# A decoder layer on TensorE: head pairs of the self-attention in three visits instead of four, and projection blocks handed out as they end

## The chip, the cores and the metric

The kernel runs on one core of a Trainium2 chip. The metric is the device time of one execution in microseconds, as the median of several runs; beside it stands one execution recorded by the hardware profiler. TensorE (PE) does the matmuls, VectorE (DVE) and ScalarE (ACT) the element-wise work, GpSimd (POOL) little, and SyncE (SP) issues the loads of weights.

## The reference

One trunk layer for 256 tokens of width 1024. What matters for the change:

```python
x = x + 0.5 * swiglu(rms_norm(x, g_ffn1), w_ffn1_gu, w_ffn1_down)
h = rms_norm(x, g_mix)
q, k, v = split(h @ w_in)                 # two groups: 12 heads dilated windows, 4 heads block-sparse
ya, yb = rms_norm(attention of each group)
x = x + concatenate([ya, yb]) @ w_out
# cross attention, 4 heads of width 256, over 256 memory tokens
q = rms_norm(x, g_cross) @ w_cq;  k, v = split(rms_norm(mem, g_mem) @ w_ckv)
s = einsum('bshe,bmhe->bhsm', q, k) * 256 ** -0.5
x = x + (softmax(s) @ v) @ w_co
x = x + 0.5 * swiglu(rms_norm(x, g_ffn2), w_ffn2_gu, w_ffn2_down)
return rms_norm(x, g_final)
```

With 256 tokens both kinds of self-attention come down to a causal softmax with a table of bias per head.

## The kernel before

Activations lie transposed: features on the partitions, 256 tokens along the free dimension. Every product is done in a split form: a number is a high part and a low part (the rest), both in a fast format, and a product is high x high, high x low and low x high. A weight tile of 128 x 1024 is loaded by SyncE and split by ScalarE (L125, the high part) and then VectorE (L126, the low part, which reads the high one). An activation tile is split the same way by `split` (L318 on ScalarE, L319 on VectorE).

`projT` computes a projection transposed, in blocks of 128 output features. A block takes a bank of TensorE's accumulator memory (eight banks, handed round as they come free) and pairs of input tiles: two matmuls of 512 columns (L224) and two of 256 (L228) a step. It returns the list of its banks when all blocks are done, and the caller then evicts them: `halves` adds the two halves of a bank with ScalarE (L275) and VectorE (L276).

TensorE's order is the order of the program. So that TensorE has work while a softmax runs on the other engines, the program has a clock of its own: each matmul adds an assumed time (`tick`), `later(delay, fn)` puts a piece of attention into a list, and it is written out between two matmuls of a projection as soon as this clock passes its due time. ScalarE's, VectorE's and GpSimd's orders are made by a scheduler.

Self-attention has two groups of eight heads. `attend(g)` handles a group as four pairs of heads (j = 0 to 3): `products` (scores, L516), `softmax`, `turn` (six transpositions of the weights, L555, copied out at L559 and L561) and `pv` (weights times values, L572, copied out at L575, squared for the norm at L348). Group 0 is laid over the projections of group 1 (`qkv(1)`), group 1 over the keys and values of cross attention (`cross_k`, `cross_v`). The pairs come in four visits: scores 0, 1; scores 2 with values 0; scores 3 with values 1; values 2, 3.

Cross attention: `cross_qp` computes Q in two halves of four blocks (c = 0, 1) and queues the four heads' scores (L188, L189, L190, 256 columns); `turn` transposes the weights (L706); `cross_o(h)` multiplies by the values. The output projection `addT(w_co)` starts between them: its `order` names which steps stand ahead of `cross_o(2)` and `cross_o(3)`.

Of the kernel before, what the change touches and what calls it, by code (L numbers as in the profile page):

```python
# [9 lines left out]
F32 = mybir.dt.float32  # L10
# [6 lines left out]
P = 128  # L17
# [3 lines left out]
FF = 2816  # L21
# [7 lines left out]
def layer_kernel(ctx, tc, x_in, mem_in, g_ffn1, w_gu1, w_dn1, g_mix, w_in, rel_bias, g_out_a, g_out_b,  # L29
# [16 lines left out]
    def slot(dt=F32R):  # L46
        return slp.tile([P, 1024], dt, tag="slot", name="slot")
# [83 lines left out]
    def colchunk(wd, c0, n, nkt=KT):  # L131

        per = 1024 // n
        res = []
        for k0 in range(0, nkt, per):
            nk = min(per, nkt - k0)
            w = wload((lambda raw, nk=nk: raw[:, :nk * n].rearrange("p (a n) -> p a n", n=n),
                       cols(wd, k0, nk, c0, n), nk * n))
            res += [(w, i * n) for i in range(nk)]
        return res  # L140
# [17 lines left out]
    def later(delay, fn, *args):  # L158
        events.append((clock[0] + delay, len(events_seq), fn, args))
        events_seq.append(0)  # L160
        events.sort(key=lambda e: e[:2])
# [80 lines left out]
    def projT(wk, xs, nblk, spread=False, whole=0, abreast=False):  # L242

        res = [bank() for _ in range(nblk)] if spread or abreast else []
        if spread and whole:
            res = [b[:, :256] for b in res]
            for k in range(KT):
                mmT_wide(res, wk, xs, k, k == 0, k == KT - 1)
            return res
        if spread:  # L250
            for k in range(KT):
                mmT_run([(res[blk], k, blk) for blk in range(nblk)], wk, xs, 0, KT - 1)
            return res
        if abreast:
            for b0 in range(0, nblk, 2):
                for k in range(0, KT, 2):
                    for blk in (b0, b0 + 1):
                        mmT_run([(res[blk], k, blk), (res[blk], k + 1, blk)], wk, xs, 0, KT - 1)
            return res
        for blk in range(nblk):  # L260
            b = bank()
            if blk >= nblk - whole:
                b = b[:, :256]
                for k in range(KT):
                    mmT(b, wk, xs, k, blk, k == 0, k == KT - 1)
            else:
                for k in range(0, KT, 2):
                    mmT_run([(b, k, blk), (b, k + 1, blk)], wk, xs, 0, KT - 1)
            res.append(b)
        return res  # L270

    def halves(out, ps):

        t = work.tile([P, 256], F32, tag="sq", name="hv", bufs=3)
        nc.scalar.activation(t, ps[:, 256:], AF.Copy)  # L275
        nc.vector.tensor_tensor(out, ps[:, :256], t, OP.add)  # L276
# [136 lines left out]
    def gate_up(w_gu, xs, st, hooks=(), first=None):  # L413
        hid = []
        for c in range(6):
            n = 512 if c < 5 else 256
            nb = n // P
            if c == 0 and first:
                pg, pu = first
            else:  # L420
                pg = projT(colchunk(w_gu, c * 512, n), xs, nb, spread=(c == 0))
                pu = projT(colchunk(w_gu, FF + c * 512, n), xs, nb)
            sil = []
            for b0 in range(0, nb, 2):
                g = work.tile([P, 512], F32, tag="g1", name="g1", bufs=3)
                scaled(g, pg[b0:b0 + 2], st.rows())
                nc.scalar.activation(g, g, AF.Silu)  # L427
                sil.append(g)
            for b0 in range(0, nb, 2):
                u = work.tile([P, 512], F32, tag="u1", name="u1")  # L430
                scaled(u, pu[b0:b0 + 2], st.rows())
                nc.vector.tensor_tensor(u, u, sil[b0 // 2], OP.mult)  # L432
                s = slot()
                hid.append(s)
                split(s, 0, 2, u)
            if c < len(hooks) and hooks[c] is not None:
                later(0.0, hooks[c])
        return hid
# [66 lines left out]
    def attend(g, q, k, v, OT, every, done, wait=1.0):  # L505


        pts, pTs = {}, {}

        def products(j):  # L510
            o = j * 256
            rows = (slice(0, 64), slice(64, 128))
            sp = [bank(), bank()]
            for c, n, t in ((0, 128, 0), (128, 256, 128)):
                for e in range(2):
                    nc.tensor.matmul(sp[e][:, c:c + n], q[rows[e], o + t:o + t + 128], k[rows[e], o:o + n],  # L516
                                     start=True, stop=True)
            tick(0.6)
            return sp

        def scores(js):
            sps = [products(j) for j in js]
            if js[0] > 1:
                pv(js[0] - 2)
            for j, sp in zip(js, sps):
                softmax(j, sp)
                later(12.0 if j == 1 else 8.0, turn, j)

        def softmax(j, sp):
            pts[j] = []  # L530
            for e in range(2):
                h = g * 8 + j * 2 + e
                pt = work.tile([P, 384], F32, tag="pt", name="pt", bufs=4)
                mx = small.tile([P, 2], F32, tag="mx", name="mx")
                nm = small.tile([P, 2], F32, tag="nm", name="nm")
                l = small.tile([P, 2], F32, tag="l", name="l")
                rl = small.tile([P, 2], F32, tag="rl", name="rl")
                for tb, c, n, fo in ((0, 0, 128, 128), (1, 128, 256, 0)):
                    nc.vector.tensor_tensor_reduce(pt[:, c:c + n], sp[e][:, c:c + n], F[h // 8][:, h % 8, fo:fo + n],
                                                   1.0, -3.0e38, OP.add, OP.max, mx[:, tb:tb + 1])  # L540
                nc.vector.tensor_scalar(nm, mx, -1.0, None, OP.mult)
                for tb, c, n in ((0, 0, 128), (1, 128, 256)):
                    nc.scalar.activation(pt[:, c:c + n], pt[:, c:c + n], AF.Exp, bias=nm[:, tb:tb + 1],
                                         accum_out=l[:, tb:tb + 1])
                nc.vector.reciprocal(rl, l)
                for tb, c, n in ((0, 0, 128), (1, 128, 256)):
                    nc.gpsimd.tensor_scalar(pt[:, c:c + n], pt[:, c:c + n], rl[:, tb:tb + 1], 1.0, OP.mult, OP.mult)
                pts[j].append(pt)

        def turn(j):  # L550
            pTs[j] = []
            for e in range(2):
                tp = bank()
                for i in range(3):
                    nc.tensor.transpose(tp[:, i * P:(i + 1) * P], pts[j][e][:, i * P:(i + 1) * P], ident)  # L555
                tick(0.33)
                pT = work.tile([P, 384], F32, tag=("pT", "u1")[e], name="pT", bufs=2)
                if e == 0:
                    nc.vector.tensor_copy(pT, tp[:, :384])  # L559
                else:  # L560
                    nc.scalar.activation(pT, tp[:, :384], AF.Copy)  # L561
                pTs[j].append(pT)
            if j == 3:
                later(3.2, pv, 2)
                later(3.2, pv, 3)

        def pv(j):
            op = bank()[:, :256]
            for kb, c, n in ((0, 0, 256), (1, 256, 128)):
                for e in range(2):  # L570
                    vc = kb * 512 + (j * 2 + e) * 64
                    nc.tensor.matmul(op[e * 64:e * 64 + 64, 256 - n:256], v[:, vc:vc + 64], pTs[j][e][:, c:c + n],  # L572
                                     start=kb == 0, stop=kb == 1)
            tick(0.65)
            nc.vector.tensor_copy(OT[g][:, j * 256:j * 256 + 256], op)  # L575
            done(g * 4 + j, op)

        for js, t in (((0, 1), 0.0), ((2,), 2 * every), ((3,), 2 * every + 5.0)):
            later(wait + t, scores, js)

    def out_split(OT, R, js, ot):

# [67 lines left out]
    def cross_k(ms):  # L650
        K = []
        for c in range(2):
            pieces = projT(colchunk(w_ckv, c * 512, 512), ms, 4)
            for b0 in (0, 2):
                t = work.tile([P, 512], F32, tag="g1", name="kn", bufs=3)
                for i in range(2):
                    halves(t[:, i * 256:i * 256 + 256], pieces[b0 + i])
                s = slot()
                split(s, 0, 2, t)
                K.append(s)  # L660
        return K

    V = [[None, None], [None, None]]
# [78 lines left out]
    xs = [slot() for _ in range(4)]  # L742
# [225 lines left out]
```

## Time and profile before

| | before |
|---|---|
| median of 3 runs | 610.15 us (609.44 to 610.66) |
| the profiled execution | 609.78 us, its span 607.8 us |
| granted TensorE clock, mean | 0.998 of 2.4 GHz |
| TensorE matmuls busy | 596.1 us, 98% of the span |
| VectorE busy | 434.6 us, 72% |
| ScalarE busy | 348.1 us, 57% |
| GpSimd busy | 51.6 us, 8% |

The span is what the profiler saw from the first instruction to the last; the time has some 2 us around it. Busy shares are means over stages that differ, so a stage is read from its own rows.

### The profile page before, as it was taken

The page shows a single profiled execution, that of the slowest core. Times are in us where ns is not written, and L with a number is a line of the kernel's source. Part 1 is how long each engine was busy: PE and PEld are TensorE (multiplying, and loading weights), DVE is VectorE, ACT ScalarE, POOL GpSimd, SP SyncE. Part 2 cuts the span into 40 slices and gives each one's busy share as a digit, 9 for nine tenths or more (in the row PEclk, how much of TensorE's full clock was granted, in tenths as well). Part 3 has the DMA queues.
Part 4 walks back from the last instruction along what each step waited for, and adds up shares of the span by engine and source line. Part 5 has one row for each costly group of instructions (what it writes and reads, how often), then busy time and mean ns, then how long its engine had stood idle before and what let it go on. Part 6 is the DMA issues. An engine that isn't in the chain of part 4 may idle for free.

```text
span 607.8 us, 9496 instructions
## 1 busy us (share of the span) xinstructions
PE 596.1 (98%) x3528; PEld 518.6 (85%) x3528; DVE 434.6 (72%) x730; ACT 348.1 (57%) x606; POOL 51.6 (8%) x83
## 2 busy tenths in 40 slices
PE   8999999999999999999999999899999999999995
PEld 8988888888899888888788899788888888888885
DVE  4889657887666766765797786858888787794424
ACT  6856536655645667656675565647654664654313
POOL 0000200000111102212401120003000000000000
PEclk9999999999999999999999999999999999999999
DMA  7877997677576717444445654543565566476401
GB/s 236 288 227 237 211 221 234 192 245 241 156 242 207 232 56 233 139 139 140 139 127 192 202 160 152 144 133 106 173 223 171 196 201 213 143 268 196 157 0 69
DMA packets 58989, 110.02 MB, mean 181 GB/s; under 512 B 3760, under 2 KB 14608, under 8 KB 58944
## 3 DMA queue, kind: packets, MB, share of 16 engines
q1 hardware_dynamic: 57664, 105.49, 55.1%
q0 software_dynamic: 832, 2.88, 2.8%
q10 hardware_dynamic: 448, 1.05, 0.5%
q8 instruction: 27, 0.44, 0.3%
q14 instruction: 18, 0.15, 0.1%
HBM read 107.58 MB, written 1.84 MB: 180 GB/s over the span
## 4 chain that ended last, share of the span: by engine, by line
PE 94%; DVE 2%; ACT 1%; DMA 1%; issue 1%; SPq 0%; POOLq 0%; POOL 0%; DVEq 0%
PE bank L224 43%; PE bank L228 21%; PE bank L188 7%; PE bank L190 7%; PE bank L189 7%; PE bank L238 4%; PE bank L516 1%; DMA raw<-in_w_ffn_gu_dram 1%; PE bank L555 1%; PE bank L572 1%; DVE w L126 1%; ACT w L125 1%; DVE slot L319 0%; PE bank L380 0%; PE bank L870 0%
## 5 line engine op out<-in xcount | busy, mean ns | idle before, releaser
L224 PE MATMUL bank<-slot,w 128*128 128x512 f32 x1130 | 355.0, 396 | 1.0 <-DVE slot L319 1.0
L126 DVE TENSOR_TENSOR w<-raw,w 128x1024 fp32r<-128x1024 f32 (+1 forms) x197 | 237.3, 1219 | 80.5 <-ACT w L125 79.3
L125 ACT ACTIVATE w<-raw 128x1024 fp32r<-128x1024 f32 (+1 forms) x197 | 202.5, 1051 | 89.4 <-PE bank L190 38.8
L228 PEld LDWEIGHTS bank<-slot,w 128*128 128x128 f32 x1130 | 209.7, 188 | 48.2 <-issue 0.7
L228 PE MATMUL bank<-slot,w 128*128 128x256 f32 x1130 | 221.7, 279 | 0.0
L224 PEld LDWEIGHTS bank<-slot,w 128*128 128x128 f32 x1130 | 174.2, 189 | 4.4 <-issue 1.3
L188 PE MATMUL bank<-w,slot 128*128 128x512 f32 (+1 forms) x156 | 60.5, 388 | 0.0
L190 PE MATMUL bank<-w,slot 128*128 128x512 f32 (+1 forms) x156 | 59.9, 384 | 0.0
L189 PE MATMUL bank<-w,slot 128*128 128x512 f32 (+1 forms) x156 | 59.9, 384 | 0.0
L275 ACT ACTIVATE hv<-bank 128x256 f32<-128x256 f32 x108 | 39.7, 376 | 34.0 <-PE bank L228 33.7
L190 PEld LDWEIGHTS bank<-w,slot 128*128 128x128 f32 x156 | 29.3, 188 | 6.0
L188 PEld LDWEIGHTS bank<-w,slot 128*128 128x128 f32 x156 | 29.3, 188 | 5.9 <-issue 0.3
L189 PEld LDWEIGHTS bank<-w,slot 128*128 128x128 f32 x156 | 29.3, 188 | 5.5
L238 PE MATMUL bank<-slot,w 128*128 128x256 f32 x240 | 31.6, 287 | 0.8 <-ACT w L125 0.7
L318 ACT ACTIVATE slot<-u 128x512 fp32r<-128x512 f32 x22 | 13.8, 629 | 32.0 <-DVE u L432 32.0
L238 PEld LDWEIGHTS bank<-slot,w 128*128 128x128 f32 x240 | 29.5, 191 | 1.7 <-ACT w L125 0.9
L353 POOL TENSOR_TENSOR ssq<-ssq,sq 128x256 f32<-128x256 f32 x22 | 19.5, 886 | 72.0 <-ACT sq L348 71.7
L322 DVE SCALAR_TENSOR_TENSOR slot<-X,gT,slot 128x256 fp32r<-128x256 f32 x30 | 19.4, 659 | 6.9 <-ACT slot L321 6.9
L427 ACT ACTIVATE g<-g 128x512 f32<-128x512 f32 x22 | 13.8, 631 | 18.4 <-DVE g L290 18.4
L276 DVE TENSOR_TENSOR u<-bank,hv 128x256 f32<-128x256 f32 x40 | 16.8, 421 | 9.9 <-ACT hv L275 9.8
L276 DVE TENSOR_TENSOR g<-bank,hv 128x256 f32<-128x256 f32 x40 | 16.5, 420 | 9.0 <-ACT hv L275 9.0
L321 ACT ACTIVATE slot<-X,gT 128x256 fp32r<-128x256 f32 x30 | 14.8, 506 | 13.0 <-DVE X L301 13.0
(129 smaller groups left out, 494.0 us busy)
## 6 DMA issues: line engine op xcount, KB each, us to landing
raw<-in_w_ffn_gu_dram SPq DMA_DIRECT2D x88, 512.0 KB, 4.7
raw<-in_w_ffn_down_dram SPq DMA_DIRECT2D x44, 512.0 KB, 4.6
raw<-in_w_ckv_dram SPq DMA_DIRECT2D x16, 512.0 KB, 6.0
raw<-in_w_in_dram SPq DMA_DIRECT2D x12, 512.0 KB, 3.8
raw<-in_w_in_dram SPq DMA_DIRECT2D x24, 256.0 KB, 4.4
raw<-in_w_out_dram SPq DMA_DIRECT2D x8, 512.0 KB, 5.0
raw<-in_w_cq_dram SPq DMA_DIRECT2D x8, 512.0 KB, 5.2
raw<-in_w_co_dram SPq DMA_DIRECT2D x8, 512.0 KB, 4.0
```

Source lines behind the costliest of these rows:

```text
L125: nc.scalar.activation(w[:, 0, a:b], raw[:, a:b], AF.Copy)
L126: nc.vector.tensor_tensor(w[:, 1, a:b], raw[:, a:b], w[:, 0, a:b].bitcast(F32), OP.subtract)
L188: nc.tensor.matmul(ps, ah, bh, start=start, stop=False)
L189: nc.tensor.matmul(ps, al, bh, start=False, stop=False)
L190: nc.tensor.matmul(ps, ah, bl, start=False, stop=stop)
L224: nc.tensor.matmul(ps, w[:, 0, o + blk * P:o + (blk + 1) * P], both(xs, k), start=k == first, stop=False)
L228: nc.tensor.matmul(ps[:, :256], w[:, 1, o + blk * P:o + (blk + 1) * P], both(xs, k)[:, :256], start=False, stop=k == last)
L238: nc.tensor.matmul(ps, w[:, wp_, o + blk * P:o + (blk + 1) * P], a, start=start and i == 0, stop=stop and i == 2)
L275: nc.scalar.activation(t, ps[:, 256:], AF.Copy)
L276: nc.vector.tensor_tensor(out, ps[:, :256], t, OP.add)
L322: nc.vector.scalar_tensor_tensor(l, src, g, h.bitcast(F32), OP.mult, OP.subtract)
L353: (eng or nc.gpsimd).tensor_tensor(new, self.ss, sq, OP.add)
```

## The change

The last branch of `projT` becomes a generator, `each`, which yields a block's bank when that block's matmuls are written; a caller that loops over it writes the block's eviction ahead of the next block's matmuls. That holds for the keys of group 0, queries and keys of group 1, the keys of cross attention (`cross_k` is written as such a loop), the second halves of both output projections, and Q's second half in `cross_qp`. `gate_up` takes a list of it, as before. In `attend` the pairs come in three visits: scores 0, 1; scores 2, 3 with values 0, 1; values 2, 3. The turn of a pair is due 8.5 (even pairs) or 12.5 (odd pairs) behind its softmax instead of 8.0 (12.0 for pair 1).

```diff
--- before.py
+++ after.py
@@ -257,6 +257,9 @@
                     for blk in (b0, b0 + 1):
                         mmT_run([(res[blk], k, blk), (res[blk], k + 1, blk)], wk, xs, 0, KT - 1)
             return res
+        return each(wk, xs, nblk, whole)
+
+    def each(wk, xs, nblk, whole):
         for blk in range(nblk):
             b = bank()
             if blk >= nblk - whole:
@@ -266,8 +269,7 @@
             else:
                 for k in range(0, KT, 2):
                     mmT_run([(b, k, blk), (b, k + 1, blk)], wk, xs, 0, KT - 1)
-            res.append(b)
-        return res
+            yield b
 
     def halves(out, ps):
 
@@ -418,8 +420,8 @@
             if c == 0 and first:
                 pg, pu = first
             else:
-                pg = projT(colchunk(w_gu, c * 512, n), xs, nb, spread=(c == 0))
-                pu = projT(colchunk(w_gu, FF + c * 512, n), xs, nb)
+                pg = list(projT(colchunk(w_gu, c * 512, n), xs, nb, spread=(c == 0)))
+                pu = list(projT(colchunk(w_gu, FF + c * 512, n), xs, nb))
             sil = []
             for b0 in range(0, nb, 2):
                 g = work.tile([P, 512], F32, tag="g1", name="g1", bufs=3)
@@ -521,10 +523,11 @@
         def scores(js):
             sps = [products(j) for j in js]
             if js[0] > 1:
-                pv(js[0] - 2)
+                for j in js:
+                    pv(j - 2)
             for j, sp in zip(js, sps):
                 softmax(j, sp)
-                later(12.0 if j == 1 else 8.0, turn, j)
+                later(8.5 + 4.0 * (j % 2), turn, j)
 
         def softmax(j, sp):
             pts[j] = []
@@ -575,8 +578,8 @@
             nc.vector.tensor_copy(OT[g][:, j * 256:j * 256 + 256], op)
             done(g * 4 + j, op)
 
-        for js, t in (((0, 1), 0.0), ((2,), 2 * every), ((3,), 2 * every + 5.0)):
-            later(wait + t, scores, js)
+        later(wait, scores, (0, 1))
+        later(wait + 2 * every + 2.0, scores, (2, 3))
 
     def out_split(OT, R, js, ot):
 
@@ -650,14 +653,14 @@
     def cross_k(ms):
         K = []
         for c in range(2):
-            pieces = projT(colchunk(w_ckv, c * 512, 512), ms, 4)
-            for b0 in (0, 2):
-                t = work.tile([P, 512], F32, tag="g1", name="kn", bufs=3)
-                for i in range(2):
-                    halves(t[:, i * 256:i * 256 + 256], pieces[b0 + i])
-                s = slot()
-                split(s, 0, 2, t)
-                K.append(s)
+            for blk, ps in enumerate(projT(colchunk(w_ckv, c * 512, 512), ms, 4)):
+                if blk % 2 == 0:
+                    t = work.tile([P, 512], F32, tag="g1", name="kn", bufs=3)
+                halves(t[:, (blk % 2) * 256:(blk % 2) * 256 + 256], ps)
+                if blk % 2:
+                    s = slot()
+                    split(s, 0, 2, t)
+                    K.append(s)
         return K
 
     V = [[None, None], [None, None]]
```

What this does to the order is seen on TensorE in the visits of group 1. First, before: the visit of scores 2 and values 0, one matmul of projection, then the turn of pair 1. L516 are scores, L572 values, L555 a turn, L224 and L228 the projection.

```order
L516 MATMUL bank<-slot 128x128 x2
L516 MATMUL bank<-slot 128x256 x2
L572 MATMUL bank<-pT,slot 64x256 x2
L572 MATMUL bank<-pT,slot 64x128 x2
L224 MATMUL bank<-slot,w 128x512
L555 MATMUL bank<-ident,pt 128x128 x6
L224 MATMUL bank<-slot,w 128x512
L228 MATMUL bank<-slot,w 128x256 x2
```

And with the change (L558, L518 and L575 are the same three lines):

```order
L224 MATMUL bank<-slot,w 128x512 x2
L558 MATMUL bank<-ident,pt 128x128 x6
L518 MATMUL bank<-slot 128x128 x2
L518 MATMUL bank<-slot 128x256 x2
L518 MATMUL bank<-slot 128x128 x2
L518 MATMUL bank<-slot 128x256 x2
L575 MATMUL bank<-pT,slot 64x256 x2
L575 MATMUL bank<-pT,slot 64x128 x2
L575 MATMUL bank<-pT,slot 64x256 x2
L575 MATMUL bank<-pT,slot 64x128 x2
L228 MATMUL bank<-slot,w 128x256 x2
```

The turn of pair 1 has moved ahead of the visit, and the visit holds the scores of two pairs and the values of two pairs, where before the second of each followed later.

The second place is cross attention, TensorE too. Before, behind the last matmuls of `cross_o(1)` (bank_4170), the output projection starts (bank_4210), and the scores of head 2 (bank_4216, from Q's slot_4128) stand behind two of its matmuls:

```order
L188 MATMUL bank_4170<-slot_4115,slot_3443 128x256
L189 MATMUL bank_4170<-slot_4115,slot_3443 128x256
L190 MATMUL bank_4170<-slot_4115,slot_3443 128x256
L224 MATMUL bank_4210<-slot_4167,w_4192 128x512 x2
L188 MATMUL bank_4216<-slot_3316,slot_4128 128x256
L189 MATMUL bank_4216<-slot_3316,slot_4128 128x256
L190 MATMUL bank_4216<-slot_3316,slot_4128 128x256
L188 MATMUL bank_4216<-slot_3316,slot_4128 128x256
```

With the change, the scores of head 2 (bank_4114, then bank_4133; from slot_3985) stand inside the projection of Q's block 2 (bank_4091):

```order
L228 MATMUL bank_4091<-slot_3546,w_3960 128x256 x2
L224 MATMUL bank_4091<-slot_3547,w_3965 128x512 x2
L188 MATMUL bank_4114<-slot_3247,slot_3985 128x256
L189 MATMUL bank_4114<-slot_3247,slot_3985 128x256
L190 MATMUL bank_4114<-slot_3247,slot_3985 128x256
L188 MATMUL bank_4114<-slot_3247,slot_3985 128x256
L189 MATMUL bank_4114<-slot_3247,slot_3985 128x256
L190 MATMUL bank_4114<-slot_3247,slot_3985 128x256
```

and the scores of head 3 (bank_4229, from slot_4162, which holds Q's blocks 2 and 3) directly behind `cross_o(1)` (bank_4208):

```order
L188 MATMUL bank_4208<-slot_4157,slot_3443 128x256
L189 MATMUL bank_4208<-slot_4157,slot_3443 128x256
L190 MATMUL bank_4208<-slot_4157,slot_3443 128x256
L188 MATMUL bank_4229<-slot_3319,slot_4162 128x256
L189 MATMUL bank_4229<-slot_3319,slot_4162 128x256
L190 MATMUL bank_4229<-slot_3319,slot_4162 128x256
L188 MATMUL bank_4229<-slot_3319,slot_4162 128x256
L189 MATMUL bank_4229<-slot_3319,slot_4162 128x256
```

The scores of head 2 went ahead of the end of Q, those of head 3 to the place where those of head 2 had been, without the projection's two matmuls ahead.

The third place is VectorE beside it. Before, Q's last block (bank_4103, hq_4148) is combined and split (slot_4141) ahead of the weight split w_4452:

```order
L276 TENSOR_TENSOR hq_4142<-bank_4078,hv_4143 128x256
L126 TENSOR_TENSOR w_4447<-raw_4445,w_4447 128x1024
L319 TENSOR_TENSOR slot_4141<-hq_4142,slot_4141 128x256
L276 TENSOR_TENSOR hq_4148<-bank_4103,hv_4149 128x256
L319 TENSOR_TENSOR slot_4167<-bank_4154,slot_4167 128x2x256
L319 TENSOR_TENSOR slot_4141<-hq_4148,slot_4141 128x256
L126 TENSOR_TENSOR w_4452<-raw_4450,w_4452 128x1024
L319 TENSOR_TENSOR slot_4183<-bank_4170,slot_4183 128x2x256
```

With the change (bank_4169, hq_4186, slot_4162):

```order
L126 TENSOR_TENSOR w_4442<-raw_4440,w_4442 128x1024
L321 TENSOR_TENSOR slot_4162<-hq_4163,slot_4162 128x256
L126 TENSOR_TENSOR w_4447<-raw_4445,w_4447 128x1024
L278 TENSOR_TENSOR hq_4186<-bank_4169,hv_4187 128x256
L321 TENSOR_TENSOR slot_4205<-bank_4192,slot_4205 128x2x256
L126 TENSOR_TENSOR w_4452<-raw_4450,w_4452 128x1024
L321 TENSOR_TENSOR slot_4162<-hq_4186,slot_4162 128x256
```

The low half of Q's last block now stands behind w_4452.

## Rows read from the trace of the kernel before

**Rows 1.** The page, busy us, share of the span, instructions, by engine.
```profile
PE 596.1 (98%) x3528; PEld 518.6 (85%) x3528; DVE 434.6 (72%) x730; ACT 348.1 (57%) x606; POOL 51.6 (8%) x83
```

**Rows 2.** Windows: busy us of each engine, granted clock, DMA; two stretches of 20 us.
```profile
280.00:300.00 20.00, 18.84 (x124) 15.20 (x123) 13.30 (x44) 13.20 (x40) 8.06 (x16) 1.00 0.43 136
...
380.00:400.00 20.00, 17.87 (x125) 16.27 (x124) 15.69 (x35) 12.28 (x25) 0.00 (x0) 1.00 0.45 132
```

**Rows 3.** Waits of TensorE: us in total, times, longest; three of six.
```profile
PE bank L555 <- ACT sq L348: 1.2, 1, 1.2
PE bank L224 <- DVE slot L319: 1.0, 1, 1.0
...
PE bank L188 <- ACT slot L318: 0.7, 1, 0.7
```

**Rows 4.** Timeline of TensorE: start, us, line, operands, count; score and value runs.
```profile
247.19 0.93 PE L516 MATMUL bank<-slot 64*128 64x128 f32 x8
248.05 0.87 PE L572 MATMUL bank<-pT,slot 128*64 128x256 f32 x8
...
266.85 1.52 PE L572 MATMUL bank<-pT,slot 128*64 128x256 f32 x16
...
275.80 1.58 PE L516 MATMUL bank<-slot 64*128 64x128 f32 x16
```

**Rows 5.** Timeline of TensorE, group 1: a turn without a wait and the late one.
```profile
285.31 0.39 PE L224 MATMUL bank<-slot,w 128*128 128x512 f32 x1
285.55 0.81 PE L555 MATMUL bank<-ident,pt 128*128 128x128 f32 x6
286.12 0.48 PE L224 MATMUL bank<-slot,w 128*128 128x512 f32 x1
...
289.82 0.50 PE L224 MATMUL bank<-slot,w 128*128 128x512 f32 x1
291.49 0.84 PE L555 MATMUL bank<-ident,pt 128*128 128x128 f32 x6 [1.16 <-ACT sq L348]
```

**Rows 6.** Timeline of VectorE (DVE) and ScalarE (ACT) beside the late turn.
```profile
286.07 0.56 DVE L559 COPY pT<-bank 128x384 f32<-128x384 f32 x1 [3.73 <-PE bank L555]
286.65 3.73 DVE L126 TENSOR_TENSOR w<-raw,w 128x1024 fp32r<-128x1024 f32 x3
...
290.50 0.42 DVE L575 COPY slot<-bank 128x256 f32<-128x256 f32 x1
...
290.96 0.38 ACT L348 ACTIVATE sq<-bank 128x256 f32<-128x256 f32 x1 [1.08 <-DVE slot L575]
```

**Rows 7.** Timeline of TensorE in cross attention: the three late starts.
```profile
383.60 0.28 PE L189 MATMUL bank<-slot 128*128 128x256 f32 x1
383.71 0.28 PE L190 MATMUL bank<-slot 128*128 128x256 f32 x1
385.00 0.73 PE L224 MATMUL bank<-slot,w 128*128 128x512 f32 x2 [1.00 <-DVE slot L319]
...
392.18 0.60 PE L706 MATMUL bank<-ident,cpt 128*128 128x128 f32 x4
393.47 0.39 PE L188 MATMUL bank<-slot 128*128 128x256 f32 x1 [0.69 <-ACT slot L318]
393.69 0.28 PE L189 MATMUL bank<-slot 128*128 128x256 f32 x1
394.42 0.39 PE L190 MATMUL bank<-slot 128*128 128x256 f32 x1 [0.45 <-DVE slot L319]
```

**Rows 8.** Timeline of VectorE and ScalarE in cross attention.
```profile
375.68 0.42 DVE L276 TENSOR_TENSOR hq<-bank,hv 128x256 f32<-128x256 f32 x1
...
382.45 1.22 DVE L126 TENSOR_TENSOR w<-raw,w 128x1024 fp32r<-128x1024 f32 x1
...
384.25 0.69 DVE L319 TENSOR_TENSOR slot<-bank,slot 128x512 fp32r<-128x512 f32 x1
...
378.62 1.06 ACT L125 ACTIVATE w<-raw 128x1024 fp32r<-128x1024 f32 x1 [0.31 <-PE bank L228]
```

## The prediction

> **What bounds the kernel now.** I read the page's busy times first: TensorE's matmuls fill 596.1 of 607.8 us [rows 1]. Such a kernel gets faster in two ways only: TensorE has less to do, or it stops waiting somewhere. So the second view is TensorE's busy time in stretches of 20 us. Behind the start and before the end two are not full: from 280 to 300 there are 1.16 us missing, from 380 to 400 2.13 us [rows 2]. The third view, TensorE's list of waits, says what was awaited: in the first stretch L555, a transposition of attention weights, for ScalarE's L348; in the second three matmuls for a split of an operand on VectorE or ScalarE (L319, L318) [rows 3]. Both stretches lie in what the change rearranges. The granted clock is 1.00 in both and stays out of the sum.
>
> Next to an idle time the profile's rows also start late, so I take what a wait costs from the distance of starts, less what the same rows take without a wait.
>
> **One visit fewer in each group.** The number of instructions is the same; only runs get longer. Eight score matmuls of a pair show 0.93 us, sixteen in one run 1.58; eight value matmuls 0.87, sixteen 1.52 [rows 4]. Two pairs in one run save 2 x 0.93 - 1.58 = 0.28 and 2 x 0.87 - 1.52 = 0.22 us, 0.50 together. A visit also has a switch from projection and back, which one row can't give: I allow 0 to 0.15 and take 0.05, since a visit goes away but the turn that stood beside one may stand alone. So 0.55 for a group, bounds 0.4 and 0.65; **two groups: 1.1 us**.
>
> **The stall of group 1.** Before, turn(1) stands one matmul behind scores 2 and values 0. That matmul, L224, starts at 289.82 and the turn at 291.49, 1.67 us later, where 0.24 (L224 at 285.31 to the turn at 285.55) and 0.1 for the switch would do: 1.33 us lost [rows 5]. Rows 6 say why. The bank that the turn takes is that of values 0: VectorE copies it out at 290.50, when its run of three weight splits (from 286.65, 3.73 us) is done, and ScalarE squares it at 290.96. In the new order turn(1) heads the joint visit, ahead of scores 2, 3 and values 0, 1, and needs no bank that this visit fills. What is late next? First, values 0 take the bank of the group's last key block, whose eviction still stands behind the same three splits on VectorE and ends near 290.9. The visit starts near 290.0; after a turn (0.57 [rows 5]) and 1.58 of scores it asks for that bank at 292.2: slack 1.3 us. Second, values 1 need turn(1)'s copies, which had a stretch of projection for cover and now have the scores and values 0. VectorE's copy (0.56 [rows 6]) can end near 291.4, values 1 start near 292.9: slack 1.5. So I cost the new waits at nothing: **1.33 us saved**, bounds 0 (the wait comes back at another bank) and 1.5.
>
> **Cross attention.** Before, three starts are late [rows 7]: L190 at 383.71 to L224 at 385.00 is 1.29 instead of 0.11 (383.60 to 383.71), so 1.18; the four transposes at 392.18 to L188 at 393.47 are 1.29 instead of 4 x 0.095 = 0.38 (0.57 for six in rows 5), so 0.91; L189 at 393.69 to L190 at 394.42 is 0.73, so 0.62. With some 0.1 behind the first two each, 2.9 us. The first is the output projection waiting for the split of cross_o(0)'s result, which VectorE does at 384.25 behind the weight split of 382.45 [rows 8]; the others are cross_o(2) right behind its turn. In the new order scores(2) stands inside the Q projection, and behind turn(2) come nine matmuls of cross_o(1), scores(3) and 24 of the projection ahead of cross_o(2). The projection, which needs cross_o(0)'s split, comes 3 us after cross_o(0)'s last matmul. So all three go.
>
> But scores(3) may not be ready. I let the queues run with row durations. Scores(2), twelve matmuls of 0.11 to 0.12, and turn(1) now stand ahead of block 3 of Q, so what hangs on its first step comes 1.4 + 0.45 us later: weight split w_4442 on ScalarE, released at 378.62 by L228 [rows 8], starts near 380.5, and behind the softmax of scores(2) and block 2's eviction, which also wait for scores(2), near 381.1. Scores(3) comes near 385.7 by TensorE's own rows; its fourth and fifth matmul (386.1, 386.2) need the high and the low half of the last Q block. ScalarE goes through w_4442 (1.06 [rows 8]) to 382.1, a Q split, w_4447 to 383.4, the last Q block's eviction to 383.8, w_4452, cross_o(0), w_4457 to 386.3, and the high half to 386.6. VectorE follows: w_4442 (1.22 [rows 8]) from 382.1, a Q split, w_4447 to 384.8, Q's last block, cross_o(0) (0.69), w_4452 to 387.1, and only then the low half, to 387.5, or 387.8 with something for each hand-over. So TensorE would wait 1.3 to 1.6 us at scores(3)'s fifth matmul; I take 1.5, and 0.1 behind it. **Net 2.9 - 1.6 = 1.3 us**, bounds 0 (a wait as long as the three old ones) and 2.9 (none).
>
> The Trainium skill, page TensorE: Matmul & The Clock Gate, section "Architectural detail", says that TensorE can pull weight loads ahead of matmuls in flight while VectorE and ScalarE take their queues strictly in order. By that rule VectorE can't take the last Q block's low half ahead of w_4452, and the wait stays; if it could, the sum would be 1.6 us better. Rows 7 and 8 agree as far as they go: the 1.00 us idle ended with a split that stood behind a weight split.
>
> **Blocks handed out earlier elsewhere.** Key and query blocks of the groups, cross keys, the last blocks of both output projections: each block's eviction is written ahead of the next block's matmuls. No instruction is added, SyncE's queue of loads keeps its order, and on GpSimd only two additions of squares trade places. TensorE has no wait in these stretches (those of the list that aren't in rows 3 or 7 are at the start and at L238), and a reader comes at least a block behind. I cost it at nothing; if that cover were gone, it is a queue of up to 3.73 us [rows 6].
>
> **The sum.** 1.1 + 1.33 + 1.3 = 3.7 us. The profiled execution took 609.78 us (its span and 2.0 around it); less 3.7 that is 606.1, and the runs' median, 610.15, lies 0.4 above it: 606.4. Here 0.2% is 1.2 us, about what a measurement of this kernel can tell from no change.
>
> **The rivals.** *No new wait at scores(3)*: the hand-overs are quicker than I let them be and the low half comes by 386.2. Against it: four weight splits on ScalarE and three on VectorE stand in the 6 us ahead. It gives 1.1 + 1.33 + 2.9 = 5.3, so 604.8. *A wait comes back in full*: at group 1's bank (3.7 - 1.33 = 2.4, so 607.8), or scores(3) waits as long as the three old ones (2.4 too); for it, the splits stand in the same places as before. Both give 609.0. *The change doesn't do what it says*: the longer runs lose in other switches what they gain, and the waits only move; then 609.5 to 610.7. Against it are rows 5 and 7, whose waits the new order removes by name. *Slower*: a joint visit holds two pairs' scores in four banks, two banks of values and the projection's own, of eight; they come free through VectorE, and if the softmax's reads stand behind a run of weight splits like rows 6, the next projection block waits for a bank. It decides for slower when both groups together come 3.7 + 1.2 = 4.9 us late; with the full 3.73 in each the time is 606.4 + 7.5 = 613.9. Against it: the same queue cost 1.33 in one group before and nothing in the other.
>
> **Chances and range.** The forecast (3 to 4.5 us saved) 0.58; no new wait 0.12; a wait back 0.17; no change 0.06; slower 0.07. A wait back in full at both places is within 0.2%, and I give it 0.01 of its 0.17: faster by over 0.2% 0.86, within 0.2% 0.07, slower 0.07. The range runs from the case without a wait, 604.7, to one wait back and half of a second, 608.6.
>
> **What would show it.** Right: L555's 1.2 us and the waits on L224, L188 and L190 are gone from TensorE's list; one of 1 to 2 us on a split has come at a score matmul of cross attention, the second half of scores(3); the stretch from 280 to 300 is full; runs of sixteen score and sixteen value matmuls stand side by side in both groups. Wrong: a wait of the first projection matmul behind a joint visit; or one in scores(2), whose Q block is combined at 375.68 [rows 8] and then split twice, to 376.9 at the earliest, against a need near 378.0.

## The result and the profile after

The median is 605.96 us (605.48 to 607.13, 6 runs) against 610.17 us (609.44 to 610.66, 6 runs): the ratio is 0.9934, 95% interval 0.9921 to 0.9947, so the change made the kernel 0.5 to 0.8% faster. The forecast was 606.4. The profiled execution took 605.48 us.

The page of the kernel after, its span and busy times, to be set beside [rows 1]:

```profile
span 603.7 us, 9507 instructions
...
PE 595.4 (99%) x3528; PEld 519.9 (86%) x3528; DVE 435.5 (72%) x730; ACT 348.2 (58%) x606; POOL 51.9 (9%) x83
```
The span is 4.1 us shorter, and the matmuls' busy time only 0.7. Most of the gain is waiting that went. The two stretches of [rows 2] after the change:

```profile
280.00:300.00 20.00, 20.00 (x136) 16.98 (x136) 14.68 (x46) 14.20 (x41) 7.75 (x18) 1.00 0.37 116
380.00:400.00 20.00, 19.33 (x132) 17.55 (x131) 14.39 (x24) 11.36 (x20) 0.00 (x0) 1.00 0.52 158
```
From 280 to 300 nothing is missing any more; from 380 to 400 there are 0.67 us missing instead of 2.13. TensorE's list of waits has only two entries left, instead of six:

```profile
PE bank L770 <- POOL ident masks.py:199: 1.4, 1, 1.4
PE bank L189 <- DVE slot L321: 0.6, 1, 0.6
```
The first is the start. The second is new, and is the one the forecast put at the scores of head 3 in cross attention; L555's wait and the three of cross attention [rows 3, rows 7] are gone. The groups by line show the longer runs: the 64 score matmuls have 6.3 us of busy time instead of 6.9, the 64 value matmuls 6.1 instead of 6.5.

To see how much each stage gave, I take the starts of four instructions that stand in both programs: the first scores of group 0, the first scores of group 1, the first scores of cross attention, the last matmul of cross_o(3). Before (the second is in [rows 4]), then after, from TensorE's timeline:

```profile
232.77 1.58 PE L516 MATMUL bank<-slot 64*128 64x128 f32 x16
...
369.03 0.28 PE L188 MATMUL bank<-slot 128*128 128x256 f32 x1
...
398.85 0.28 PE L190 MATMUL bank<-slot 128*128 128x256 f32 x1
```
```profile
232.80 1.57 PE L518 MATMUL bank<-slot 64*128 64x128 f32 x15
...
275.30 0.93 PE L518 MATMUL bank<-slot 64*128 64x128 f32 x8
...
366.67 0.28 PE L188 MATMUL bank<-slot 128*128 128x256 f32 x1
...
394.75 0.28 PE L190 MATMUL bank<-slot 128*128 128x256 f32 x1
```
The distances between them, and from the last to the end of the span, for all kernels of this study (us):

| kernel | group 0 | group 1 | cross attention | rest | span |
|---|---|---|---|---|---|
| before | 43.03 | 93.23 | 29.82 | 208.95 | 607.8 |
| after | 42.50 | 91.37 | 28.08 | 208.95 | 603.7 |
| visits only | 42.50 | 91.37 | 29.82 | 208.95 | 605.3 |
| hand-out only | 43.03 | 91.89 | 28.03 | 208.94 | 604.8 |
| turn of pair 1 earlier | 43.02 | 91.90 | 29.82 | 208.94 | 607.0 |
| runs of eight | 42.83 | 91.69 | 28.05 | 208.95 | 604.4 |
| hand-out only, keys held | 43.03 | 93.24 | 28.03 | 208.93 | 605.9 |
| scores of head 3 later | 42.50 | 91.37 | 27.82 | 208.93 | 603.5 |
| Q's last block whole | 42.50 | 91.37 | 26.96 | 209.03 | 602.4 |

So the change gave 0.53 in group 0, 1.86 in group 1 and 1.74 in cross attention, 4.13 in all, and nothing behind. What is ahead of the first mark differs by up to 0.8 us between executions (the last section).

In group 1 TensorE's timeline shows the joint visit: turn of pair 1, sixteen scores, sixteen values, and back to the projection without an idle time.

```profile
289.44 0.82 PE L558 MATMUL bank<-ident,pt 128*128 128x128 f32 x6
290.19 1.58 PE L518 MATMUL bank<-slot 64*128 64x128 f32 x16
291.70 1.52 PE L575 MATMUL bank<-pT,slot 128*64 128x256 f32 x16
293.15 0.50 PE L228 MATMUL bank<-slot,w 128*128 128x256 f32 x2
```
VectorE beside it: three weight splits, then the last key block's eviction (L278), then the copy of the turned weights (L562).

```profile
286.41 3.69 DVE L126 TENSOR_TENSOR w<-raw,w 128x1024 fp32r<-128x1024 f32 x3
290.01 0.41 DVE L278 TENSOR_TENSOR kn<-bank,hv 128x256 f32<-128x256 f32 x1
290.35 0.54 DVE L562 COPY pT<-bank 128x384 f32<-128x384 f32 x1
```
The eviction ends at 290.42 and values 0 start at 291.70: if values 0 take that bank, as the forecast has it, the slack is 1.28 us, where the forecast had 1.3. The profile's rows don't tell banks apart.

### The profile page after: what moved, and what is told of

The parts are those of the page before. It is cut to its first block, busy times and chain, and to the rows that moved or that the text cites. A ratio compares the mean times of both kernels' runs of the same rounds, so it can differ in the third digit from the quotient of the medians.

```text
span 603.7 us, 9507 instructions
## 1 busy us (share of the span) xinstructions
PE 595.4 (99%) x3528; PEld 519.9 (86%) x3528; DVE 435.5 (72%) x730; ACT 348.2 (58%) x606; POOL 51.9 (9%) x83
## 4 chain that ended last, share of the span: by engine, by line
PE 92%; DVE 3%; ACT 1%; issue 1%; DMA 1%; POOL 0%; POOLq 0%; ACTq 0%; SPq 0%
PE bank L224 42%; PE bank L228 21%; PE bank L188 7%; PE bank L189 7%; PE bank L190 7%; PE bank L238 3%; DVE w L126 1%; PE bank L518 1%; PE bank L575 1%; PE bank L558 1%; DMA raw<-in_w_co_dram 1%; DVE slot L321 1%; ACT w L125 1%; ACT cpt L698 0%; PE bank L770 0%
## 5 line engine op out<-in xcount | busy, mean ns | idle before, releaser
L224 PE MATMUL bank<-slot,w 128*128 128x512 f32 x1130 | 353.7, 396 | 0.0
L228 PEld LDWEIGHTS bank<-slot,w 128*128 128x128 f32 x1130 | 209.7, 188 | 48.6 <-issue 1.0
L228 PE MATMUL bank<-slot,w 128*128 128x256 f32 x1130 | 222.5, 279 | 0.0
L224 PEld LDWEIGHTS bank<-slot,w 128*128 128x128 f32 x1130 | 174.0, 189 | 2.5 <-issue 0.6
L238 PE MATMUL bank<-slot,w 128*128 128x256 f32 x240 | 31.8, 289 | 0.0
L238 PEld LDWEIGHTS bank<-slot,w 128*128 128x128 f32 x240 | 30.0, 194 | 0.5 <-DVE slot L324 0.4
L278 DVE TENSOR_TENSOR u<-bank,hv 128x256 f32<-128x256 f32 x40 | 16.7, 418 | 8.8 <-ACT hv L277 8.7
L278 DVE TENSOR_TENSOR g<-bank,hv 128x256 f32<-128x256 f32 x40 | 16.3, 417 | 8.3 <-ACT hv L277 8.3
```

Source lines behind the costliest of these rows:

```text
L224: nc.tensor.matmul(ps, w[:, 0, o + blk * P:o + (blk + 1) * P], both(xs, k), start=k == first, stop=False)
L228: nc.tensor.matmul(ps[:, :256], w[:, 1, o + blk * P:o + (blk + 1) * P], both(xs, k)[:, :256], start=False, stop=k == last)
L238: nc.tensor.matmul(ps, w[:, wp_, o + blk * P:o + (blk + 1) * P], a, start=start and i == 0, stop=stop and i == 2)
```

## The experiments

Ratios and medians are against the kernel before, run beside it on the same chip; a wait or a place is read from the profiled execution.

**Visits only.** The edit to the kernel before is the part of the diff in `attend`, nothing else:

```diff
-                pv(js[0] - 2)
+                for j in js:
+                    pv(j - 2)
...
-                later(12.0 if j == 1 else 8.0, turn, j)
+                later(8.5 + 4.0 * (j % 2), turn, j)
...
-        for js, t in (((0, 1), 0.0), ((2,), 2 * every), ((3,), 2 * every + 5.0)):
-            later(wait + t, scores, js)
+        later(wait, scores, (0, 1))
+        later(wait + 2 * every + 2.0, scores, (2, 3))
```

> The kernel before with the three visits and the turns' due times alone; blocks are still evicted after the whole projection. Theory (the visits' terms stand by themselves: 0.55 a group by longer runs, 1.33 by the stall of group 1): 610.2 - 2.4 = 607.8, L555's wait of 1.2 gone, the three waits of cross attention still there. Rival (the values of the joint visit find their bank free only because key blocks are evicted early): a wait of 1 us or more at a value matmul or at the turn in group 1, 609.0 to 609.3.

Measured: 607.16 us against 610.05, ratio 0.9951 (0.9937 to 0.9965). Groups 0 and 1 give exactly what the whole change gives there, 0.53 and 1.86, and cross attention gives nothing; its three waits stand in the list as before:

```profile
PE bank L224 <- DVE slot L319: 1.0, 1, 1.0
PE bank L188 <- ACT slot L318: 0.7, 1, 0.7
PE bank L190 <- DVE slot L319: 0.4, 1, 0.4
```
The theory holds: the joint visit needs no key block handed out early. The rival is met in another way, though, and not refuted: VectorE takes the first key blocks out of their banks (L276) 10 us earlier here than in the kernel before, although the program still writes their eviction behind all four blocks. First this kernel, then before:

```profile
281.81 0.76 DVE L276 TENSOR_TENSOR kn<-bank,hv 128x256 f32<-128x256 f32 x2
```
```profile
291.81 0.42 DVE L276 TENSOR_TENSOR kn<-bank,hv 128x256 f32<-128x256 f32 x1
```
The joint visit is due later than the visit of scores 2 was, and here the fourth key block is done ahead of it (ScalarE copies it at 288.40, the turn starts at 289.31). With the whole change the first two key blocks are taken out at 281.95, as far behind the first mark as here (49.15 us): with the visits in, the keys' hand-out moves nothing.

**Hand-out only.** The kernel after, with `attend` as before (the edit above, backwards).

> The kernel with the change, but with the four visits and due times of before. Theory (the hand-out acts in cross attention alone, 2.9 less a wait of 1.2 at scores of head 3): 610.2 - 1.7 = 608.5, L555's wait on L348's successor still there with about 1.2 us. Rival (early eviction of the keys also clears the queue in front of group 1's turn): that wait is gone too and the time is 607.1.

Measured: 606.73 us against 610.05, ratio 0.9942 (0.9930 to 0.9955). Cross attention gives 1.79, as the theory says. But group 1 gives 1.34 as well, with four visits and the old due times: the rival is right. TensorE in group 1 of this kernel, values 0, one matmul of projection, the turn:

```profile
289.17 0.87 PE L574 MATMUL bank<-pT,slot 128*64 128x256 f32 x8
289.97 0.50 PE L224 MATMUL bank<-slot,w 128*128 128x512 f32 x1
290.30 0.82 PE L557 MATMUL bank<-ident,pt 128*128 128x128 f32 x6
```
and VectorE's splits and its copy (L577) of the bank of values 0:

```profile
286.75 3.72 DVE L126 TENSOR_TENSOR w<-raw,w 128x1024 fp32r<-128x1024 f32 x3
...
290.60 0.42 DVE L577 COPY slot<-bank 128x256 f32<-128x256 f32 x1
```
The order on TensorE is that of before, the three splits stand where they stood, and the bank of values 0 is copied out only at 290.60; yet the turn starts at 290.30, 0.33 behind the matmul ahead. So it no longer takes the bank of values 0. By then three key blocks have left their banks, two in this row and the third at 285.44:

```profile
282.60 0.76 DVE L278 TENSOR_TENSOR kn<-bank,hv 128x256 f32<-128x256 f32 x2
```

**Hand-out only, keys held.** Which of the handed-out blocks frees the bank? The last kernel, with `cross_k` back at holding its four blocks:

```diff
-            for blk, ps in enumerate(projT(colchunk(w_ckv, c * 512, 512), ms, 4)):
...
+            pieces = list(projT(colchunk(w_ckv, c * 512, 512), ms, 4))
+            for b0 in (0, 2):
...
```

> The kernel of the run with the hand-out alone (four visits), but the keys of cross attention are held until all four blocks are done, as before. Theory (with the keys handed out, a key block's bank is free when turn(1) asks for one, so it need not take that of values 0): the turn's wait of about 1.2 us on ScalarE's square is back, 606.7 + 1.3 = 608.0. Rival (another hand-out, of group 1's queries and keys, moved the banks): no such wait, 606.7.

Measured: 608.09 us against 610.19, ratio 0.9970 (0.9958 to 0.9982). The wait is back, and group 1 takes 93.24 again:

```profile
289.72 0.50 PE L224 MATMUL bank<-slot,w 128*128 128x512 f32 x1
291.39 0.84 PE L557 MATMUL bank<-ident,pt 128*128 128x128 f32 x6 [1.17 <-ACT sq L350]
```
The first key block leaves its bank only behind the turn's start:

```profile
291.71 0.42 DVE L278 TENSOR_TENSOR kn<-bank,hv 128x256 f32<-128x256 f32 x1
```
So it is the keys of cross attention: handed out as they end, their banks are free when the turn asks for one. Cross attention still takes 28.03, so its gain isn't the keys'; by the code it is left to Q's second half, which no run hands out alone.

**Turn of pair 1 earlier.** One number in the kernel before:

```diff
-                later(12.0 if j == 1 else 8.0, turn, j)
+                later(10.5 if j == 1 else 8.0, turn, j)
```

> The kernel before with one number changed: the turn of pair 1 due 10.5 instead of 12.0 behind its softmax, so that in both groups it stands ahead of scores 2 and values 0, while the visits stay four. Theory (the turn waited for the bank of values 0, which stood ahead of it): the wait goes, 610.2 - 1.2 to 1.4 = 608.9. Rival (VectorE's three weight splits hold TensorE up wherever the turn stands, at the next bank): the wait comes at another matmul with about 1 us, and the time stays 609.8 to 610.3.

Measured: 608.65 us against 610.05, ratio 0.9977 (0.9967 to 0.9987). Group 1 gives 1.33, group 0 nothing. The turn stands directly ahead of scores 2 now, and neither it nor the visit waits:

```profile
288.51 0.82 PE L555 MATMUL bank<-ident,pt 128*128 128x128 f32 x6
289.26 0.93 PE L516 MATMUL bank<-slot 64*128 64x128 f32 x8
```
The stall was the order of turn and values on one bank, and turning it round is enough: no key block leaves its bank here before 294.57. VectorE's run is another one in this kernel (two splits from 287.20, the turn's copy at 289.71, then the third split), so that a run of three holds nothing up by itself is shown by the hand-out alone, where it stood unchanged and TensorE didn't wait.

**Runs of eight.** In the kernel after, inside the joint visit:

```diff
-            sps = [products(j) for j in js]
-            if js[0] > 1:
-                for j in js:
+            sps = []
+            for j in js:
+                sps.append(products(j))
+                if js[0] > 1:
                     pv(j - 2)
```

> The kernel with the change, but inside the joint visit the order is scores 2, values 0, scores 3, values 1: no projection between, yet runs of eight. Theory (the gain of 0.5 a group is that of the run: a switch from scores to values and back costs about 0.2 each): 0.4 a group lost, 606.0 + 0.8 = 606.8. Rival (the gain is the visit's way from and to the projection): 606.0 to 606.2.

Measured: 606.55 us against 610.05, ratio 0.9942 (0.9929 to 0.9954). The intervals of this kernel and the one after overlap, so the marks decide: 0.33 in group 0 and 0.32 in group 1 are lost. The visit of group 1:

```profile
290.61 0.93 PE L518 MATMUL bank<-slot 64*128 64x128 f32 x8
291.46 0.87 PE L576 MATMUL bank<-pT,slot 128*64 128x256 f32 x8
292.26 0.93 PE L518 MATMUL bank<-slot 64*128 64x128 f32 x8
293.12 0.87 PE L576 MATMUL bank<-pT,slot 128*64 128x256 f32 x8
```
From 290.61 to 292.26 and again behind it, each pair takes about 1.65 us (the projection goes on at 293.92); sixteen and sixteen took 2.96 (290.19 to 293.15). Of the 0.53 that group 0 gains, 0.33 is the longer run and 0.20 the visit that is gone. Both theories named a part; the longer run is the larger, and 0.07 a group less than expected.

**Scores of head 3 later.** In the kernel after, the due time of one piece:

```diff
-                    later(3.0 + 3.0 * (blk // 2) * (c == 0), scores, c * 2 + blk // 2)
+                    later(4.0 if c and blk == 3 else 3.0 + 3.0 * (blk // 2) * (c == 0), scores, c * 2 + blk // 2)
```

> The kernel with the change, but head 3's scores due 4.0 instead of 3.0 behind the Q projection, so that five matmuls of the output projection (1.1 us by their rows) stand between cross_o(1) and them. Theory (the wait at scores(3) is lateness of Q's last block and any work fills it): 1.2 us less, and 0.2 lost by the projection's first matmul, whose operand VectorE ends at 383.41 against 383.2, and up to 0.5 at cross_o(3), whose turn has only six matmuls behind it: 605.2, between 604.8 and 605.6. Rival (the wait only moves, to the projection and cross_o(3)): 605.8 to 606.3.

Measured: 605.33 us against 610.19, ratio 0.9922 (0.9908 to 0.9935). By the marks cross attention gives only 0.26 of the 1.2. The wait at the scores is gone, but TensorE's timeline has two other late starts, the output projection's first matmul and cross_o(3):

```profile
383.42 0.28 PE L190 MATMUL bank<-slot 128*128 128x256 f32 x1
383.68 0.74 PE L224 MATMUL bank<-slot,w 128*128 128x512 f32 x2
384.26 0.40 PE L228 MATMUL bank<-slot,w 128*128 128x256 f32 x2
...
392.89 0.28 PE L189 MATMUL bank<-slot 128*128 128x256 f32 x1
393.39 0.38 PE L190 MATMUL bank<-slot 128*128 128x256 f32 x1 [0.23 <-DVE slot L321]
```
0.26 from 383.42 and 0.58 from 383.68 where 0.12 and 0.46 would do, 0.50 from 392.89 and 0.23 behind it where 0.12 each would do: 0.75 in all; of the remaining 0.2 (1.2 - 0.26 - 0.75), 0.11 lies ahead of the edit, at the scores of head 2: their fourth matmul starts at 375.56, the sixth at 375.93, 0.37 us where 0.25 passed after the change. The low half of their Q block ends at 375.66 and the fifth matmul starts at 375.71. The last 0.1 isn't placed. The median lies where the theory put it, but the marks say that most of the wait moved. The rival is nearer.

**Q's last block whole.** In the kernel after:

```diff
-... projT(colchunk(w_cq, c * 512, 512), xs, 4, spread=(c == 0), whole=4 * (c == 0)) ...
+... projT(colchunk(w_cq, c * 512, 512), xs, 4, spread=(c == 0), whole=(4, 1)[c]) ...
```

> The kernel with the change, but Q's last block is computed in 24 matmuls of 256 columns (as the output projections' last blocks are) instead of 8 of 512 and 8 of 256, so it needs no adding of halves and its low half stands ahead of w_4452 on VectorE. Theory (scores(3) waits because that low half is behind w_4452): the low half is done near 382.7 against a need near 383.8, the wait of 1.2 is gone, 0.1 for 24 x 0.12 in place of 2.78: 604.9. Rival (the high half on ScalarE, or the matmuls themselves, are what is late): a wait of 0.5 us or more stays, 605.6 to 606.0.

Measured: 604.33 us against 610.19, ratio 0.9906 (0.9892 to 0.9919), the fastest of all. VectorE of this kernel: a weight split, two splits of activations, the next weight split:

```profile
380.92 1.22 DVE L126 TENSOR_TENSOR w<-raw,w 128x1024 fp32r<-128x1024 f32 x1
382.05 1.04 DVE L321 TENSOR_TENSOR slot<-bank,slot 128x256 fp32r<-128x256 f32 x2
383.01 1.22 DVE L126 TENSOR_TENSOR w<-raw,w 128x1024 fp32r<-128x1024 f32 x1
```
Q's low half is the first of the two in the row of 382.05; it stands ahead of the weight split of 383.01, and scores(3)'s fifth matmul starts without an idle time. The list of waits holds the start alone.

Cross attention takes 26.96, 1.12 less than after the change, as expected: 1.2 for the wait and 0.1 back for the block's other form. The wait at scores(3) was lateness of Q's last block. The block's form does several things at once, though: its low half is ahead of a weight split on VectorE, ScalarE's copy and VectorE's adding of the halves are gone, and ScalarE makes the high half at 380.54 instead of 383.49 after the change. So the rival that named the high half is not refuted by this run, and no run parts these; the rows of the kernel after do in part (next section).

## Why the prediction was right, point by point

**Longer runs.** 0.55 a group, measured 0.53 in group 0 and, beside the stall, 1.86 - 1.33 = 0.53 in group 1. The sum held, its parts did not: the longer runs are worth 0.33 (runs of eight), where the durations gave 0.50, and the visit that is gone 0.20, where the guess was 0.05. The 0.50 was too large since rows reach past the next row's start: by starts the visit's sixteen and sixteen save 2 x 1.65 - 2.96 = 0.34. Two errors of about the same size cancelled, and that is luck.

**The stall of group 1.** 1.33, measured 1.33 with the turn of pair 1 earlier and 1.34 with the hand-out alone. The cause was right: the turn asked for the bank of values 0, behind VectorE's splits. What the step missed is that the change removes it in more than one way. The order is enough (the turn earlier), key blocks out of their banks early are enough (the hand-out alone), and the joint visit brings both, since it comes behind the fourth key block; no run parts them there. "Blocks handed out earlier elsewhere: nothing" is right for the sum, but only since the other half of the change had taken the stall already. The keys' hand-out is worth 1.34 by itself, and nothing once the visits are in; the gains of the two halves in group 1, 1.86 and 1.34, give 1.86 together.

**Cross attention.** 2.9 for the three waits: all three went. The new wait was put at the right matmuls, the fourth and fifth of scores(3), but too long: 1.6 with what lies behind it, measured 1.2. The rows, TensorE:

```profile
383.59 0.28 PE L190 MATMUL bank<-slot 128*128 128x256 f32 x1
383.99 0.38 PE L188 MATMUL bank<-slot 128*128 128x256 f32 x1
384.93 0.39 PE L189 MATMUL bank<-slot 128*128 128x256 f32 x1 [0.55 <-DVE slot L321]
385.15 0.28 PE L190 MATMUL bank<-slot 128*128 128x256 f32 x1
```
1.56 us from 383.59 to 385.15 where 0.36 would do. VectorE in front of it:

```profile
379.76 1.23 DVE L126 TENSOR_TENSOR w<-raw,w 128x1024 fp32r<-128x1024 f32 x1 [0.26 <-ACT w L125]
380.90 0.42 DVE L321 TENSOR_TENSOR slot<-hq,slot 128x256 fp32r<-128x256 f32 x1
381.24 1.22 DVE L126 TENSOR_TENSOR w<-raw,w 128x1024 fp32r<-128x1024 f32 x1
...
383.32 1.22 DVE L126 TENSOR_TENSOR w<-raw,w 128x1024 fp32r<-128x1024 f32 x1
384.45 0.42 DVE L321 TENSOR_TENSOR slot<-hq,slot 128x256 fp32r<-128x256 f32 x1
```
The low half (384.45) is behind the weight split (383.32), as the working had it (w_4452), and the splits ran as early as it said (the first is at 379.76, the forecast's 382.1 less the 2.36 by which cross attention begins earlier, 369.03 to 366.67). What was too long is the sum of durations: the splits stand 1.13 to 1.14 us from the next row's start, though their rows show 1.22, and nothing is lost from hand to hand. So the term was 1.3 and is 1.74, all of it in this one wait.

VectorE's queue is not the whole of it. ScalarE of the kernel after, a weight split and then the high half of Q's last block:

```profile
382.55 1.09 ACT L125 ACTIVATE w<-raw 128x1024 fp32r<-128x1024 f32 x1
383.49 0.44 ACT L320 ACTIVATE slot<-hq 128x256 fp32r<-128x256 f32 x1
```
The high half ends at 383.93, and the fourth matmul starts at 383.99, 0.28 late. The low half reads the high one, so it could not start before 383.93 either; it did at 384.45. With VectorE free at 383.93 the fifth matmul would come some 0.5 us earlier, not 1.2 (an estimate from these rows): to take the whole wait away both halves must come earlier, as they do in Q's last block whole. The Trainium skill (TensorE: Matmul & The Clock Gate, section "Architectural detail") says that VectorE takes its queue strictly in order. The rows agree: the low half's operands were there at 383.93, and it starts 1.13 us behind the weight split ahead of it in the queue.

What the working had as safe, scores(2), was close. It gave them 1.1 us (376.9 against 378.0); after the change the low half of their Q block ends at 375.44 and the fifth matmul starts at 375.60, 0.16 later, mostly because the block is combined 0.8 us later behind the start of cross attention than before (374.12 - 366.67 against 375.68 - 369.03). That no wait came there is in part luck: with the scores of head 3 later, 0.11 us were lost at this place.

**The sum.** 3.7 forecast, 4.13 between the marks. The rivals: no wait at scores(3) didn't come (it takes one more edit), group 1's bank didn't come back, and the slower side had no sign: behind both joint visits the projection goes on at once. The ends of the range don't quite follow from their cases: without a wait it is 610.15 - 5.33 = 604.8 (604.7 stands there), and one wait back and half of a second some 608.4 (608.6); neither bears on the result.

## What to carry to other kernels

Two edits that each remove the same stall are to be tried one by one, or the second one looks free and worthless; here the visits alone gave 2.39 between the marks, the hand-out alone 3.13, and both together 4.13. A queue on an engine that is 72% busy can still end last: where both halves of an operand's split stood behind weight splits, a form with fewer steps ahead of them (the whole block, 24 matmuls at 0.1 us more) took the wait away, while filling it with other work moved most of it on. And a short wait is priced from starts: distance of starts, less the distance without a wait.

## What the runs showed of the hardware that had not been expected

The stages repeat far better than the whole: the part behind cross attention took 208.93 to 208.95 us in eight of nine kernels and 209.03 in the ninth (its end, the span, is read to 0.1), and a group or cross attention that an edit doesn't touch is the same to 0.05. What scatters is the start: the first mark lies between 232.54 and 233.32. A matmul of the first projection (L238) waits there for a weight split for 0 to 1.06 us from one profiled execution to the next, but that wait alone doesn't set the mark: it is 0.69 before and none after, and the marks are 232.77 and 232.80. Why the start scatters stays open. Differences of a few tenths are to be read between marks, not from spans.

VectorE's rows overlap: a weight split of 1.22 us is followed by the next row's start 1.13 to 1.14 us behind its own.
